# A two-layer attention trunk on one core: hand-ordered vector and scalar queues in the value projection, two of four weight sums added in place by the vector engine

## The chip, the core and the metric

One core of a Trainium2 chip runs the whole program. Its engines work side by side and each takes its own instructions in order: TensorE (PE) multiplies, with weight loads shown as PEld; VectorE (DVE) and ScalarE (ACT) do elementwise work and read the result memory (PSUM); GpSimd (POOL) does elementwise work on SBUF alone and issues accumulating DMAs; SyncE (SP) issues the plain DMAs. The metric is the device time of one execution in microseconds. Everything is float32, multiplied as float32r in two parts: each operand is split into a high part (`hi`, a rounding copy by ACT) and a rest (`lo` = source - `hi`, a subtraction by DVE or POOL), and a product is hi*hi + lo*hi + hi*lo.

## What is computed

Two encoder layers over 512 tokens of width 1024. The stretch at hand is the input projection of the first layer's neighbourhood attention:

```python
xn = rmsnorm(x, norm_g[0])
q, k, v, z = jnp.split(xn @ w_in, 4, axis=-1)     # each 512 x 1024
o = neighbourhood_attention(q, k, v, rpb)          # 16 heads of 64
y = (o * silu(z)) @ w_out
h = x + y
x = h + sigmoid(rmsnorm(h, ple_norm[0]) @ ple_w_gate[0]) * (p[0] @ ple_w_proj[0])
```

The second layer has latent attention in place of `mixer_na`, and a last norm follows.

## The kernel before, in words

`run` first makes `xs` (the transposed, scaled input, in the two tiles `xk[0]` and `xk[1]` of four row blocks each) and its split `xT` (`xh` and `xl`, L1124 to L1128): for each row block DVE scales, ACT copies `xh`, and the rest `xl` is DVE's for the first four blocks and POOL's for the last four. The gate columns `z` come in between (L176, L177). `load_w` (L82 to L84) brings a weight by SP, copies its high part on ACT (`wwhi`) and takes its rest on POOL (`wwlo`).

`values_seven` computes v = xn @ w_v by seven half-size products in place of eight (Strassen's scheme in Winograd's manner, 256 tokens by 512 columns each, in two row halves i). Product p multiplies a left operand by a weight quarter or by a sum of quarters. Products 1, 2 and 4 take `xT` itself. The left operands of 7, 5, 6 and 3 are mixes of `xs`: L1137 adds or subtracts halves of `xk` in place (`d`, by DVE), ACT copies the high part (`h`, L1140) and DVE takes the rest (`l`, L1141). The weights of products 7, 6, 4 and 5 are sums of quarters (T1, T2): a plain DMA brings one quarter and accumulating DMAs, issued by POOL (L248), add the others, W7 = q(1,0) + q(1,2), then W6 = W7 + q(0,0) and W4 = W6 + q(0,2) in the same tile; T2 becomes W5 = q(1,0) + q(0,0). `piece` (L225 to L231) splits half a weight: `whi` by ACT (L229), `wlo` by DVE in two instructions (L231). Raw pieces share three slots (`wraw`) with the weights of `load_w`, and so do the split ones (`whi`, `wlo`).

Each product is 24 matmuls of 128x128 by 128x512 (L277). Products share banks of PSUM: 2 accumulates on 1, 5 and 3 on 6, 4 on 7. So ACT must copy product 1 (`s1`, L285) before product 2 begins; product 7 is added to `s1` and copied to `s17`, product 6 is copied to `s6` and subtracted from 7, and `v_split` (L94, L96) splits finished quarters into the tiles Q. Between the products stand the queries and keys of the first two head pairs: `early(j)`, 48 matmuls (L338), whose results `queries` (ACT L344 and L345, DVE L346 to L353) and `keys` (four copies by ACT, L362 to L365, two rests by DVE, L366 and L367) bring into SBUF.

On PE the order of projection and products is written out: each matmul follows `last_mm`. The sequence is pair 0, product 1, product 2, pair 1, products 7, 6, 4, 5, 3. On ACT, DVE, POOL and SP a planner orders the instructions by its own time model, each engine taking what it reckons ready, earlier source lines first. `issue_after(x)` puts an instruction behind x on its engine.

Of the kernel before, what the change touches and what calls it, by code (L numbers as in the profile page):

```python
# [39 lines left out]

class Trunk:
    def __init__(self, tc, ctx, a, dbg=None):
# [3 lines left out]
        ec = ctx.enter_context  # L46
        self.const = ec(tc.tile_pool(name="const", bufs=1))
# [44 lines left out]
    def split(self, hi, lo, src, scale=1.0):  # L92
        nc = self.nc
        self.last_copy = nc.scalar.activation(hi, src, AF.Copy, scale=scale)  # L94
        if scale == 1.0:
            nc.vector.tensor_tensor(out=lo, in0=src, in1=hi.bitcast(F32), op=ALU.subtract)  # L96
        else:
            nc.vector.scalar_tensor_tensor(lo, src, scale, hi.bitcast(F32), op0=ALU.mult, op1=ALU.subtract)
# [125 lines left out]
    def piece(self, pool, raw, own):  # L224

        nc = self.nc
        hi, lo = ((self.wp if own else pool).tile([P, 1024], F32R, name=t, tag=t if own else "vw", bufs=3 if own else 4)
                  for t in ("whi", "wlo"))
# [5 lines left out]
    def raw_piece(self, n, c, after=None):  # L234
        raw = self.wp.tile([P, 1024], F32, name="wraw", tag="wraw", bufs=3)
        with self.tc.issue_after(after.ins) if after else nullcontext():
            self.nc.sync.dma_start(raw, self.a["na_v"][n, c])
        return raw

    def values_seven(self, pool, xT, X, Q, piece, project):  # L240
# [3 lines left out]
        T = pool.tile([P, 2, 1024], F32, name="T1", bufs=1)  # L244
        first = nc.sync.dma_start(T, quarter(1, 0))
        pool.tile([P, 1024], F32R, name="vw", tag="vw", bufs=4)
        T2 = pool.tile([P, 2, 1024], F32, name="T2", bufs=1)
        add = lambda t, n, c: nc.gpsimd.dma_start(t, quarter(n, c), accum_op=ALU.add, max_dma_last_dim=4096)  # L248
        add(T, 1, 2)
        W, C, s1, s17, s6 = {1: [piece]}, {}, {}, {}, {}  # L250
        made = lambda raw, own: self.piece(pool, raw, own)
# [9 lines left out]
        sub = lambda o, x, y: nc.vector.tensor_tensor(out=o, in0=x, in1=y, op=ALU.subtract)  # L261

        def out(th, n, i, ps):
            self.v_split(Q[th, n][:, 2 * i:2 * i + 2, :], ps)

        def product(p):
            for i in range(2):
                if p in banks:
                    C[p, i] = self.psum(banks[p])
            steps = [(c, i) for c in range(2) for i in range(2)] if p == 1 else [(c, i) for i in range(2) for c in range(2)]  # L270
            for c, i in steps:
                ps = C[base.get(p, p), i]
                m = [(left(p, s, k, i), W[p][c][r][:, k % 2 * S:(k % 2 + 1) * S])
                     for s, r in ((0, 0), (1, 0), (0, 1)) for k in (2 * c, 2 * c + 1)]
                for j, (l, r) in enumerate(m):
                    with self.tc.issue_after(self.last_mm.ins):
                        self.last_mm = nc.tensor.matmul(ps, l, r, start=c == 0 and j == 0 and p in banks,  # L277
                                                        stop=c == 1 and j == 5 and p in (2, 3, 4), skip_group_check=True)
                if c:
                    done(p, i, ps)  # L280

        def done(p, i, ps):
            if p == 1:
                s1[i] = self.temp("s1")
                nc.scalar.activation(s1[i], ps, AF.Copy)  # L285
            elif p == 2:
                out(0, 0, i, ps)
            elif p == 7:
                nc.vector.tensor_tensor(out=ps, in0=ps, in1=s1[i], op=ALU.add)
                s17[i] = pool.tile([P, S], F32, name="s17", tag="s", bufs=3)  # L290
                nc.scalar.activation(s17[i], ps, AF.Copy)
            elif p == 6:
                s6[i] = pool.tile([P, S], F32, name="s6", tag="s", bufs=3)
                nc.scalar.activation(s6[i], ps, AF.Copy)
                sub(C[7, i], C[7, i], s6[i])
            elif p == 4:
                out(1, 0, i, ps)
            elif p == 5:
                q = self.psum("O" if i else "T")
                sub(q, ps, s17[i])  # L300
                sub(ps, ps, s1[i])
                out(1, 1, i, q)
            else:
                out(0, 1, i, ps)

        project(0)
        W[1].append(made(self.raw_piece(0, 1, first), False))
        W[2] = [made(self.raw_piece(0, 2 + c), True) for c in range(2)]
        product(1)
        project(1, True)  # L310
        W[7] = [made(T[:, c, :], c) for c in range(2)]
        product(2)
        add(T, 0, 0)
        project(1, False)
        W[6] = [made(T[:, c, :], True) for c in range(2)]
        product(7)
        add(T, 0, 2)
        nc.sync.dma_start(T2, quarter(1, 0))
        add(T2, 0, 0)
        W[4] = [made(T[:, c, :], False) for c in range(2)]  # L320
        product(6)
        W[5] = [made(T2[:, c, :], True) for c in range(2)]
        product(4)
        W[3] = [made(self.raw_piece(1, 2 + c), not c) for c in range(2)]
        product(5)
        product(3)

    def na_heads(self, pool, xT, zs, Q, XV, weights, piece):
        nc, a = self.nc, self.a
        A, U = {}, {}  # L330

        def load(j):
            weights[j] = [self.load_w(a["na_qk"][i + j], 1024) for i in (0, 8)]
# [7 lines left out]
        def queries(psq):  # L341
            sa = pool.tile([P, S], F32R, name="sa", tag="qs", bufs=4)
            sb = pool.tile([P, S], F32R, name="sb", tag="qs", bufs=4)
            nc.scalar.activation(sa[0:64], psq[0:64], AF.Copy, scale=0.125)  # L344
            nc.scalar.activation(sb[64:128], psq[64:128], AF.Copy, scale=0.125)  # L345
            nc.vector.scalar_tensor_tensor(sa[64:128], psq[0:64], 0.125, sa[0:64].bitcast(F32),  # L346
                                           op0=ALU.mult, op1=ALU.subtract)
            nc.vector.scalar_tensor_tensor(sb[0:64], psq[64:128], 0.125, sb[64:128].bitcast(F32),
                                           op0=ALU.mult, op1=ALU.subtract)
            s0 = []  # L350
            for s in (sa, sb):
                e0 = pool.tile([P, P], F32R, name="s0", tag="s0", bufs=4)
                nc.vector.tensor_copy(e0.rearrange("p (a b) -> p a b", a=2),  # L353
                                      win(s, 0, P, 0, [[448, 2], [1, 64]]).bitcast(F32))
                s0.append(e0)
            return (sa, sb), s0

        def keys(j, psk):
# [3 lines left out]
            nc.scalar.activation(da[0:64], psk[0:64], AF.Copy)  # L362
            nc.scalar.activation(da[64:128], psk[0:64], AF.Copy)
            nc.scalar.activation(db[64:128], psk[64:128], AF.Copy)
            nc.scalar.activation(db[0:64], psk[64:128], AF.Copy)  # L365
# [1013 lines left out]
```

## Time and profile before

| | us |
|---|---|
| median of 3 runs (lowest, highest) | 671.32 (670.32, 671.85) |
| the profiled execution | 669.5 |
| its span, first to last instruction | 667.7 |
| PE busy | 646.0 (97%) |
| DVE, ACT, POOL busy | 429.7, 452.1, 422.2 |

The profile is of one execution. In its timeline a row merges neighbouring instructions of one kind; its second number is the time from the first one's start to the last one's end. Matmuls are pipelined, so eight of them issued every 0.2 us show as one row with the last one's own length at its end. The idle time before a row stands in brackets with what ended it.

### The profile page before, as it was taken

To read this page: it belongs to the slowest core of one execution; us is meant where nothing else is said; L and a number is where in the kernel's file an instruction comes from. 1 tells how busy PE (TensorE), PEld (TensorE's weight loads), DVE (VectorE), ACT (ScalarE), POOL (GpSimd) and SP (SyncE) were. 2 spreads that over 40 slices of the span, in tenths; PEclk is the share of its full clock that TensorE was granted. 3 is DMA by queue.
4 is the path that set the end of the run, shared out by engine and by line. 5 is a ranking of instruction groups with operands and counts; after the bars stand their busy time and mean duration, and the time that the engine had idled before them with its cause. 6 is when DMAs were issued, how large, how long until landed. Compare 5 with 4: busy or idle time off the path is not lost.

```text
span 667.7 us, 9952 instructions
## 1 busy us (share of the span) xinstructions
PE 646.0 (97%) x3299; PEld 543.5 (81%) x3299; DVE 429.7 (64%) x890; ACT 452.1 (68%) x887; POOL 422.2 (63%) x379
## 2 busy tenths in 40 slices
PE   9988987999999999999999999999999999999994
PEld 6866865888888888888899888888888888888884
DVE  6297545476768634567851823788888886374675
ACT  7575444688788754488755544888979898537855
POOL 0493400587987865389844744685978978436974
PEclk9998997999999999999999999999999999999998
DMA  9846853498996898646643425320122213584524
GB/s 323 341 158 189 220 95 94 143 251 209 240 252 168 220 217 257 233 152 200 211 126 122 139 79 142 96 67 9 56 64 64 64 48 132 187 323 132 171 82 158
DMA packets 46100, 107.41 MB, mean 161 GB/s; under 512 B 4705, under 2 KB 17761, under 8 KB 46049
## 3 DMA queue, kind: packets, MB, share of 16 engines
q1 hardware_dynamic: 34032, 85.02, 37.8%
q0 software_dynamic: 11584, 20.97, 15.5%
q10 hardware_dynamic: 432, 0.79, 0.3%
q8 instruction: 26, 0.43, 0.3%
q14 instruction: 26, 0.21, 0.1%
HBM read 95.23 MB, written 25.17 MB: 180 GB/s over the span
## 4 chain that ended last, share of the span: by engine, by line
PE 83%; DMA 8%; ACT 2%; DVE 2%; issue 2%; POOL 2%; POOLq 0%; SPq 0%; DVEq 0%; ACTq 0%
PE ps_mm L107 27%; PE ps_S L107 10%; PE ps_mm L855 7%; PE ps_T L139 6%; PE ps_T L747 5%; PE ps_O L967 4%; PE ps_mm L747 3%; PE ps_S L747 3%; DMA T<-na_v 3%; PE ps_O L504 2%; PE ps_T L107 2%; PE ps_O L107 2%; DMA wraw<-na_z 2%; PE ps_mm L805 2%; PE ps_mm L277 2%
## 5 line engine op out<-in xcount | busy, mean ns | idle before, releaser
L84 POOL TENSOR_TENSOR wwlo<-wraw,wwhi 128x1024 fp32r<-128x1024 f32 (+5 forms) x70 | 123.2, 1772 | 75.2 <-ACT wwhi L83 67.5
L692 POOL TENSOR_TENSOR wlo<-wraw,whi 128x512 fp32r<-128x512 f32 x56 | 72.9, 1335 | 22.3 <-ACT whi L690 20.3
L952 POOL TENSOR_TENSOR ex<-ex,rc 128x512 f32<-128x512 f32 x64 | 66.3, 1043 | 25.8 <-DVE rc L951 21.7
L83 ACT ACTIVATE wwhi<-wraw 128x1024 fp32r<-128x1024 f32 (+5 forms) x73 | 57.1, 805 | 30.6 <-PE ps_mm L107 13.5
L950 ACT ACTIVATE ex<-ps_S,mx 128x512 f32<-128x512 f32 x64 | 44.0, 688 | 11.7 <-DVE mx L948 10.1
L948 DVE TENSOR_REDUCE mx<-ps_S 128x1 f32<-128x512 f32 x64 | 43.7, 683 | 8.2 <-PE ps_S L107 7.5
L96 DVE TENSOR_TENSOR pt_lo<-ps_T,pt_hi 128x512 fp32r<-128x512 f32 x64 | 43.2, 682 | 7.1 <-ACT pt_hi L94 6.7
L478 POOL TENSOR_TENSOR ex<-ex,rc 128x128 f32<-128x128 f32 (+1 forms) x64 | 36.0, 637 | 13.7 <-DVE rc L474 13.7
L94 ACT ACTIVATE pt_hi<-ps_T 128x512 fp32r<-128x512 f32 x64 | 37.7, 595 | 3.3 <-PE ps_T L139 3.0
L139 PE MATMUL ps_T<-ident,ex 128*128 128x128 f32 x256 | 38.3, 272 | 0.0
L139 PEld LDWEIGHTS ps_T<-ident,ex 128*128 128x128 f32 x256 | 31.5, 140 | 7.5
L472 ACT ACTIVATE ex<-ex,mx 128x128 f32<-128x128 f32 (+1 forms) x64 | 30.2, 473 | 9.4 <-DVE mx L462 6.7
L107 PE MATMUL ps_mm<-xh,wwhi 128*128 128x512 f32 x120 | 32.5, 400 | 0.0
L107 PE MATMUL ps_mm<-xh,wwlo 128*128 128x512 f32 x120 | 32.2, 396 | 0.0
L107 PE MATMUL ps_mm<-xl,wwhi 128*128 128x512 f32 x120 | 32.1, 397 | 0.0
L690 ACT ACTIVATE whi<-wraw 128x1024 fp32r<-128x1024 f32 x28 | 29.3, 1056 | 3.2 <-DMA wraw<-sum 2.0
L209 POOL TENSOR_TENSOR u<-u,z 128x512 f32<-128x512 f32 x16 | 22.0, 1372 | 14.4 <-DVE u L205 10.4
L205 DVE TENSOR_TENSOR u<-ps_O,u 64x512 f32<-64x512 f32 x32 | 21.9, 685 | 13.8 <-ACT u L204 13.3
L107 PE MATMUL ps_S<-ko,qo 128*128 128x512 f32 x96 | 28.9, 409 | 0.0
L107 PE MATMUL ps_S<-ke,qe 96*128 96x512 f32 x96 | 28.6, 406 | 0.0
L855 PE MATMUL ps_mm<-cT,wwhi 128*128 128x512 f32 x94 | 27.7, 393 | 0.0
L204 ACT ACTIVATE u<-ps_O 64x512 f32<-64x512 f32 x32 | 19.0, 593 | 12.4 <-PE ps_O L504 9.1
(473 smaller groups left out, 1930.6 us busy)
## 6 DMA issues: line engine op xcount, KB each, us to landing
sum<-gate POOLq DMA_DIRECT2D x12, 1024.0 KB, 8.6
wraw<-na_qk SPq DMA_DIRECT2D x16, 512.0 KB, 4.7
wraw<-sum SPq DMA_DIRECT2D x16, 512.0 KB, 3.3
pe<-pe SPq DMA_DIRECT2D x31, 256.0 KB, 6.1
wraw<-gate SPq DMA_DIRECT2D x12, 512.0 KB, 3.3
T<-na_v POOLq DMA_DIRECT2D x4, 1024.0 KB, 8.9
sum<-sum POOLq DMA_DIRECT2D x4, 1024.0 KB, 10.7
wraw<-na_o SPq DMA_DIRECT2D x8, 512.0 KB, 4.7
```

The lines of the kernel that those rows point to most:

```text
L83: nc.scalar.activation(hi[:, c], raw[:, c], AF.Copy)
L84: f = lambda e, c=c: e.tensor_tensor(out=lo[:, c], in0=raw[:, c], in1=hi[:, c].bitcast(F32), op=ALU.subtract)
L94: self.last_copy = nc.scalar.activation(hi, src, AF.Copy, scale=scale)
L96: nc.vector.tensor_tensor(out=lo, in0=src, in1=hi.bitcast(F32), op=ALU.subtract)
L107: last = self.last_mm = nc.tensor.matmul(out, l, r, start=i == 0, stop=i == n - 1)
L139: self.last_mm = self.nc.tensor.transpose(t[:, i * P:(i + 1) * P], b, self.ident)
L692: nc.gpsimd.tensor_tensor(out=lo[:, o], in0=raw[:, o], in1=hi[:, o].bitcast(F32), op=ALU.subtract)
L747: mm = nc.tensor.matmul(ps, l, r, start=j == 0 and p in banks, stop=j == 11 and p in (2, 3, 4), skip_group_check=True)
L855: self.last_mm = nc.tensor.matmul(PS[key], *terms[i], start=i == 0, stop=i == len(terms) - 1)
L948: nc.vector.reduce_max(mx, sp, axis=AX.X, negate=True)
L950: nc.scalar.activation(ex, sp, AF.Exp, bias=mx, accum_out=sm)
L952: nc.gpsimd.tensor_tensor(out=ex, in0=ex, in1=rc.to_broadcast([P, S]), op=ALU.mult)
```

## The change

- `values_seven` and the query and key steps within it issue their ACT and DVE operations through `InOrder`, which puts each one behind the one before it in the source. `load_w`, POOL's work and the DMAs are not chained. Afterwards the planner orders these engines as before.
- The steps are written out in one sequence (below). The mixes move from `run` into it, spread between the weight pieces, and all stand ahead of `after1`, the copy of product 1. `mix` and `piece` start with ACT's copy and return the rest as a later step.
- W7 and W5 are still made by a plain and an accumulating DMA each. W6 and W4 are made by DVE, which adds raw pieces to W7's tile in place (`sums`), after plain DMAs have brought the pieces.
- `xl` of the last four row blocks is DVE's too.
- The sequence of products ends 7, 6, 5, 4, 3. A pair's queries and keys get both banks first, and `queries` and `keys` are steps of their own. Every product runs by weight halves first, then by row halves.
- The tiles of `xs` and of the raw input lie in the pool `nav`, in the memory that the results Q take later: `more()` makes the two Q tiles that replace `xs`, after the last mix. The other memory at the start of the stretch shifts accordingly.

```diff
+class InOrder:
+    def __init__(self, tc, engine):
+        self.tc, self.engine, self.last = tc, engine, None
+    def __getattr__(self, name):
+        call = getattr(self.engine, name)
+        def run(*args, **kw):
+            with self.tc.issue_after(self.last.ins) if self.last is not None else nullcontext():
+                self.last = call(*args, **kw)
+            return self.last
+        return run
...
-    def piece(self, pool, raw, own):
+    def piece(self, pool, raw):
...
-        nc.scalar.activation(hi, raw, AF.Copy)
-        for o in (slice(0, S), slice(S, 2 * S)):
-            nc.vector.tensor_tensor(out=lo[:, o], in0=raw[:, o], in1=hi[:, o].bitcast(F32), op=ALU.subtract)
-        return hi, lo
+        self.act.activation(hi, raw, AF.Copy)
+        return lambda: [self.rest(hi, lo, raw, o) for o in (slice(0, S), slice(S, 2 * S))] and (hi, lo)
...
+    def mix(self, xk, p):
+        lo, hi = slice(0, 2 * P), slice(2 * P, S)
+        d, y, op = {7: ((0, lo), (0, hi), ALU.subtract), 5: ((0, hi), (1, hi), ALU.subtract),
+                    6: ((1, hi), (0, lo), ALU.add), 3: ((1, lo), (1, hi), ALU.subtract)}[p]
+        d, y = (xk[g][:, :, c] for g, c in (d, y))
+        self.dve.tensor_tensor(out=d, in0=d, in1=y, op=op)
+        t = self.bigtile(f"V{p}")
+        h, l = (t[:, 2 * s:2 * s + 2, :].rearrange("p a (b c) -> p (a b) c", b=2) for s in range(2))
+        self.act.activation(h, d, AF.Copy)
+        return t, lambda: self.dve.tensor_tensor(out=l, in0=d, in1=h.bitcast(F32), op=ALU.subtract)
...
+        def load(p, n, c):
+            T[p] = pool.tile([P, 2, 1024], F32, name=f"W{p}", bufs=1)
+            nc.sync.dma_start(T[p], quarter(1, 0))
+            nc.gpsimd.dma_start(T[p], quarter(n, c), accum_op=ALU.add, max_dma_last_dim=4096)
+        load(7, 1, 2)
...
+        sums = lambda t, i, raw: self.dve.tensor_tensor(out=t[:, i, :], in0=t[:, i, :], in1=raw, op=ALU.add)
...
+        made(1, 0, self.raw_piece(0, 0))
+        rest7 = mixed(7)
+        made(1, 1, self.raw_piece(0, 1), True)
+        load(5, 0, 0)
+        rest7()
+        made(2, 0, self.raw_piece(0, 2))
+        pair.products(0)
+        pair.queries(0)
+        rest5 = mixed(5)
         product(1)
+        p21 = self.piece(None, self.raw_piece(0, 3))
+        rest5()
+        W[2].append(p21())
+        rest6 = mixed(6)
+        pair.keys(0)
+        pair.load(1)
+        rest6()
+        mixed(3)()
+        more()
+        after1(0)
+        after1(1)
+        made(7, 0, T[7][:, 0, :], True)
         product(2)
+        out(0, 0, 0, C[1, 0])
+        out(0, 0, 1, C[1, 1])
+        made(7, 1, T[7][:, 1, :])
+        raws = [self.raw_piece(0, c) for c in both]
+        sums(T[7], 0, raws[0])
+        made(6, 0, T[7][:, 0, :], True)
+        sums(T[7], 1, raws[1])
+        pair.products(1)
+        pair.queries(1)
+        made(6, 1, T[7][:, 1, :])
+        raws = [self.raw_piece(0, 2 + c) for c in both]
+        sums(T[7], 0, raws[0])
+        sums(T[7], 1, raws[1])
+        pair.keys(1)
+        made(5, 0, T[5][:, 0, :])
         product(7)
+        made(4, 0, T[7][:, 0, :], True)
+        after7(0)
+        after7(1)
+        made(5, 1, T[5][:, 1, :])
         product(6)
+        made(4, 1, T[7][:, 1, :], True)
+        after6(0)
+        after6(1)
+        made(3, 0, self.raw_piece(1, 2))
+        product(5)
+        made(3, 1, self.raw_piece(1, 3))
+        after5(0)
+        after5(1)
         product(4)
...
-                (nc.vector, nc.gpsimd)[k // 4].tensor_tensor(out=lo, in0=xs[k], in1=hi.bitcast(F32), op=ALU.subtract)
+                nc.vector.tensor_tensor(out=lo, in0=xs[k], in1=hi.bitcast(F32), op=ALU.subtract)
```

## Rows read from the trace of the kernel before

**Rows 1.** The page: PE's busy time and share, and its granted clock in 40 slices.

```profile
PE 646.0 (97%) x3299; PEld 543.5 (81%) x3299; DVE 429.7 (64%) x890; ACT 452.1 (68%) x887; POOL 422.2 (63%) x379
...
PEclk9998997999999999999999999999999999999998
```

**Rows 2.** View by windows: stretch, busy us by engine, granted clock, DMA share, GB/s.

```profile
99.90:110.00 10.10, 5.52 (x13) 3.83 (x13) 5.52 (x9) 4.43 (x6) 0.00 (x0) 0.67 0.29 58
110.00:124.10 14.10, 14.10 (x62) 11.67 (x63) 7.35 (x11) 7.14 (x10) 5.42 (x3) 0.99 0.36 116
sum 80.20, PE 68.07 PEld 53.22 DVE 48.88 ACT 37.37 POOL 25.56; mean PE 9.72 PEld 7.60 DVE 6.98 ACT 5.34 POOL 3.65
```

**Rows 3.** View of waits, PE: total us, times, longest us.

```profile
PE ps_T L277 <- ACT whi L229: 4.6, 1, 4.6
PE ps_mm L338 <- POOL xl L1128: 4.4, 1, 4.4
PE ps_mm L277 <- DVE lb L367: 1.7, 1, 1.7
```

**Rows 4.** Timeline, PE, pair 0: start, us, engine, line, operation, tiles, count, wait.

```profile
44.12 1.98 PE L338 MATMUL ps_mm<-xh,wwhi 128*128 128x512 f32 x8
...
52.12 0.76 PE L338 MATMUL ps_mm<-xl,wwhi 128*128 128x512 f32 x1 [4.42 <-POOL xl L1128]
...
52.67 3.36 PE L338 MATMUL ps_mm<-xh,wwlo 128*128 128x512 f32 x8
...
55.87 1.98 PE L338 MATMUL ps_mm<-xh,wwhi 128*128 128x512 f32 x8
```

**Rows 5.** Timeline: the third accumulating DMA and product 4 behind it.

```profile
94.97 1.20 POOL L248 DMA_DIRECT2D T<-na_v  x1 [12.18 <-DVE wlo L231]
...
103.31 2.95 ACT L229 ACTIVATE whi<-T 128x1024 fp32r<-128x1024 f32 x3 [4.76 <-DMA T<-na_v]
...
104.42 1.22 PE L277 MATMUL ps_T<-whi,xh 128*128 128x512 f32 x2 [4.57 <-ACT whi L229]
...
109.97 0.83 PE L277 MATMUL ps_T<-whi,xh 128*128 128x512 f32 x2
```

**Rows 6.** Timeline, DVE at the beginning of the stretch.

```profile
39.53 2.49 DVE L1128 TENSOR_TENSOR xl<-xT,xh 128x512 fp32r<-128x512 f32 x4
...
44.33 0.69 DVE L176 TENSOR_TENSOR z<-ps_mm,R 128x512 f32<-128x512 f32 x1
```

**Rows 7.** Timeline, ACT and DVE: one of each step that the change queues.

```profile
42.56 1.06 ACT L229 ACTIVATE whi<-wraw 128x1024 fp32r<-128x1024 f32 x1
...
53.06 1.21 DVE L1137 TENSOR_TENSOR xT<-xT 128x1024 f32<-128x1024 f32 x1
...
54.37 1.06 ACT L1140 ACTIVATE V<-xT 128x1024 fp32r<-128x1024 f32 x1 [2.35 <-DVE xT L1137]
...
58.99 0.69 DVE L346 SCALAR_TENSOR_TENSOR sa<-ps_mm,sa 64x512 fp32r<-64x512 f32 x1
...
60.58 0.22 DVE L353 CAST s<-sb 128x128 fp32r<-128x128 f32 x1
...
61.52 0.59 ACT L362 ACTIVATE da<-ps_mm 64x512 fp32r<-64x512 f32 x1 [2.73 <-PE ps_mm L338]
...
64.66 0.69 DVE L367 TENSOR_TENSOR lb<-ps_mm,db 64x512 fp32r<-64x512 f32 x1
...
67.28 0.60 ACT L285 ACTIVATE s<-ps_S 128x512 f32<-128x512 f32 x1 [0.50 <-PE ps_S L277]
...
73.01 1.29 DVE L231 TENSOR_TENSOR wlo<-T,whi 128x512 fp32r<-128x512 f32 x2 [0.26 <-ACT whi L229]
```

**Rows 8.** Timeline, POOL and DVE at work beside each other.

```profile
40.41 6.70 POOL L1128 TENSOR_TENSOR xl<-xT,xh 128x512 fp32r<-128x512 f32 x3 [1.35 <-ACT xh L1127]
...
47.07 2.79 POOL L84 TENSOR_TENSOR wwlo<-wraw,wwhi 128x1024 fp32r<-128x1024 f32 x1
...
47.58 3.35 DVE L1137 TENSOR_TENSOR xT<-xT 128x1024 f32<-128x1024 f32 x1
```

More of the change, by code (lines that the diff above doesn't have):

```diff
@@ L242, in values_seven @@
+    def values_seven(self, pool, xT, xk, Q, pair, more):
         nc = self.nc
         quarter = lambda n, c: self.a["na_v"][n, c:c + 2].rearrange("c p n -> p c n")
[L244 to L248, printed above, removed]
@@ L269, in product @@
                     C[p, i] = self.psum(banks[p])
[L270 to L304, printed above, removed]
@@ L306, in values_seven @@
-        project(0)
-        W[1].append(made(self.raw_piece(0, 1, first), False))
-        W[2] = [made(self.raw_piece(0, 2 + c), True) for c in range(2)]
-        product(1)
-        project(1, True)
-        W[7] = [made(T[:, c, :], c) for c in range(2)]
-        product(2)
-        add(T, 0, 0)
-        project(1, False)
-        W[6] = [made(T[:, c, :], True) for c in range(2)]
+            for c in range(2):
+                for i in range(2):
+                    ps = C[base.get(p, p), i]
+                    m = [(left(p, s, k, i), W[p][c][r][:, k % 2 * S:(k % 2 + 1) * S])
+                         for s, r in ((0, 0), (1, 0), (0, 1)) for k in (2 * c, 2 * c + 1)]
+                    for j, (l, r) in enumerate(m):
+                        with self.tc.issue_after(self.last_mm.ins):
+                            self.last_mm = nc.tensor.matmul(ps, l, r, start=c == 0 and j == 0 and p in banks,
+                                                            stop=c == 1 and j == 5 and p in (2, 3, 4),
+                                                            skip_group_check=True)
@@ new lines, in after7, with after6, after5 @@
+        def after7(i):
+            self.dve.tensor_tensor(out=C[7, i], in0=C[7, i], in1=s1[i], op=ALU.add)
+            s17[i] = copy("s17", i, C[7, i])
+        def after6(i):
+            s6[i] = copy("s6", i, C[6, i])
+            sub(C[7, i], C[7, i], s6[i])
+        def after5(i):
+            q = self.psum("O" if i else "T")
+            sub(q, C[6, i], s17[i])
+            sub(C[6, i], C[6, i], s1[i])
+            out(1, 1, i, q)
+        made = lambda p, c, raw, vw=False: W.setdefault(p, []).append(self.piece(pool if vw else None, raw)())
@@ new lines, in values_seven, with mixed @@
+        both = range(2)
+        def mixed(p):
+            X[p], rest = self.mix(xk, p)
+            return rest
+        made(1, 0, self.raw_piece(0, 0))
[7 more added lines that the diff above has]
+        rest5 = mixed(5)
+        product(1)
+        p21 = self.piece(None, self.raw_piece(0, 3))
+        rest5()
+        W[2].append(p21())
@@ L321, in values_seven @@
         product(6)
-        W[5] = [made(T2[:, c, :], True) for c in range(2)]
+        made(4, 1, T[7][:, 1, :], True)
[6 more added lines that the diff above has]
+        after5(1)
         product(4)
-        W[3] = [made(self.raw_piece(1, 2 + c), not c) for c in range(2)]
-        product(5)
+        out(1, 0, 0, C[7, 0])
+        out(1, 0, 1, C[7, 1])
         product(3)
-    def na_heads(self, pool, xT, zs, Q, XV, weights, piece):
+        out(0, 1, 0, C[6, 0])
@@ L329, in na_heads @@
+        out(0, 1, 1, C[6, 1])
+    def na_heads(self, pool, xT, zs, Q, xk, weights, more):
         nc, a = self.nc, self.a
         A, U = {}, {}
-        def load(j):
-            weights[j] = [self.load_w(a["na_qk"][i + j], 1024) for i in (0, 8)]
         def product(out, w):
```

128 lines of the change are left out of this document (64 added, 64 removed).

## The prediction

> **What bounds the kernel now.** I read the page's engine shares first. TensorE (PE) is busy 97% of the span, and nearly all of the slices of its granted clock show full speed [rows 1]. So the other engines matter only where PE waits for them. The view by windows then shows where: in the value stretch, 43.9 to 124.1 us, PE is busy 68.07 of 80.20 us, while behind it, from 110 us on, it is busy without a gap [rows 2]. What is gained or lost has to be in the stretch, and the kernel behind it, bound by PE, passes a shift on.
>
> How much is there to gain? Eight matmuls issued back to back take 1.98 us with a last one of 0.39 [rows 4], so (1.98 - 0.39) / 7 = 0.227 us each. The stretch holds 264 of them: two pairs of 48 for queries and keys, and seven products of 24. That is 59.9 us, and with eight short score matmuls of 0.12 us (an estimate from their spacing in the trace) 60.9 us. The first starts at 44.12 us [rows 4], the last ends at about 124.0, so 79.9 - 60.9 = **19.0 us are lost**. The waits of PE name the largest: 4.4 us for POOL's `xl`, 4.6 us for ScalarE's (ACT's) `whi` [rows 3]. Each is followed by the lower of the clock's two levels (1.2 in place of 2.4 GHz; the stretch to 110 us has a granted clock of 0.67 [rows 2]). After the first, the nine matmuls from 52.12 to 55.87 us take 3.75 us where 2.0 would do [rows 4]: 1.7 lost. After the second, twelve take from 104.42 to 109.97 [rows 5], 5.55 us in place of 2.7, a short wait in it: 2.8 lost. A wait for the key rest `lb` is 1.7 [rows 3]. That makes 15.2; some 3.8 lie in smaller waits.
>
> **What the change takes away.** (a) `xl` of the last four row blocks moves from POOL to VectorE (DVE). POOL needs 6.70 us for three of them with DVE busy beside it [rows 8]; DVE makes four in 2.49 [rows 6]. DVE has made the first four by 42.0; four more and one `z` (0.69) bring it to 45.6. PE reads block 4 at about 46.9 and block 7 at 47.5, so the wait of 4.4 and its 1.7 of slow clock go. What covers the four is that the four mixes of `xk`, which follow in DVE's queue before, come later.
>
> (b) The 4.6 us are a DMA. The third accumulating transfer is issued at 94.97, when DVE has read the old sum, and ACT gets the new one at 103.31 [rows 5]. Afterwards the sums for products 6 and 4 are four DVE additions in place (1.21 us each, priced as the 128x1024 operation of L1137 [rows 7]) of pieces that plain DMAs bring ahead. The two DMA sums left, for 7 and 5, start early: their memory lies under tiles of the projection at the start, and nothing in the stretch feeds them. The additions lie in the second half, beside 16.3 us of product 2 and pair 1. So 4.6, its 2.8, and the waits of the same kind at about 91 and 97 us go.
>
> **What it adds: one order for all.** Every ACT and DVE operation of the stretch must now follow the one before it in the source. So a copy can stand behind an unrelated wait. One does: product 2 accumulates into the banks of product 1, so it must wait for the copy `s1`, and `s1` now stands on ACT behind `h3`, the high half of the last mix, which waits for DVE's `d3`. I follow both queues with uncontended durations [rows 6, 7]: a `whi` or `h` 1.06 us, a pair of `wlo` 1.29 (1.2 when the next follows directly), a mix `d` or rest `l` 1.21 (1.14 when the next follows directly, an estimate from what the pairs save), the queries' four DVE pieces 1.81 (58.99 to 60.80), four key copies of 0.59 one behind the other 2.4, then two key rests of 0.69. A hand-over from engine to engine is put at up to 0.1 us (`d6`, which begins at 53.06 and takes 1.21, to its `h` at 54.37), and the times include it.
>
> DVE is free at 45.55 us. `wlo` of W1's first piece to 46.8; `d7` 48.0; `h7` on ACT 49.1, and only then `whi` of W1's second piece, 50.1 (DVE stands 2.1 us); its `wlo` 51.4; `l7` 52.5; W2's first `wlo` 53.7; queries 55.5; `d5` 56.7; `h5` 57.9 (DVE stands 1.2); `l5` 59.1; W2's second `wlo` 60.3; `d6` 61.5; `h6` 62.6; key copies 64.9 (DVE stands 3.5, with `l6` ready behind the key rests); key rests 66.4; `l6` 67.5; `d3` 68.7; `h3` 69.8; `s1` at **70.4**.
>
> PE has no such delay: pair 0 runs 44.12 to 55.0, product 1 to 60.45. Then nothing is left for it: its own order puts product 2 next, and all other products behind. So a hole of 9.95 us opens where the trace of before has none of that size.
>
> **The unknown price** is POOL's. Its 2.4 us weight rests for pair 0's keys and pair 1's queries would fall beside DVE's `xl` and beside `d6` or `d3`. Where POOL's 2.79 us rest ran, `d5` took 3.35 us in place of 1.21 [rows 7, 8]: 2.14 each. Beside the first of POOL's `xl`, however, from 40.41 on, DVE's four took 0.62 each, undisturbed [rows 6, 8]. So the price lies between 0 and 2 x 2.14 = 4.3 us; not below 0, since the chain above has no contention in it to lose. I take half, 2.1, as the rows stand one against one. Product 2 then starts at 72.5 and the hole is 12.05 us.
>
> The Trainium skill speaks against the change here. SBUF — State Buffer, section "Who interferes with whom", states that a DVE instruction with two SBUF inputs and a GpSimd instruction that reads SBUF exclude each other for the whole of the one that came first. By that rule the full 4.3 us count; the row of `d5`, which ends 1.1 us after POOL, agrees, and the four undisturbed `xl` do not.
>
> **From product 2 on** there are 192 matmuls, 43.6 us, and 1.0 of scores. The slow clock after the hole costs 1.7 to 2.8 by the two cases of before [rows 4, 5]; I take 2.2. Following the two queues further, PE is always fed: `wlo` of W7's second piece is done some 8 us before product 7; product 6's second bank comes free, by pair 1's key rests, about 3 us before it is needed; only `s6`, behind the second `whi` of W4, comes about when product 5 wants it. I put 0.5 for such waits; both ends 0 and 3. The sum: 72.5 + 43.6 + 1.0 + 2.2 + 0.5 = 119.8 in place of 124.0, a gain of **4.2 us**. In other words, 19.0 us lost become 12.05 + 2.2 + 0.5 = 14.8.
>
> Moved at no cost: the plain loads of the four raw pieces (four of 0.5 MB in place of two accumulating transfers of 1 MB) stand in SP's queue and wait there for slots that, by the same walk, are free some 7 us ahead of use; if such a load came late, its sum would hold up ACT and DVE, which the 0.5 to 3 covers. Result tiles now lie on the mixes' source and wait for the last mix, long before the first result. Products 5 and 4 change places, with operands of both ready.
>
> The profiled execution took 669.5 us (span 667.7); less 4.2 is 665.3. The median of the three runs, 671.32, is 1.8 above it, so I forecast **667.1 us** for the median.
>
> **Rivals.** *Short hole.* The planner might let the hand order begin before `xl` of the last blocks, and fill DVE's pauses with those. DVE has 16.6 us of work from 45.55 to `d3`; without any pause `s1` would be done at 45.55 + 16.6 + 1.1 + 0.6 + 0.3 of hand-over, 64.2: a hole of 3.8. The loss is then 3.8 + 1.7 + 0.5 = 6.0, the gain 13.0, the time **658.3**. Against it: `l5` needs `h5` and the key rests need four copies on ACT; these pauses, 4.7 us, can't be filled from the chain, and only unchained work could, of which little is left.
>
> *POOL locks DVE out in full.* Product 2 starts at 70.4 + 4.3 = 74.7, the loss is 14.25 + 2.7 = 17.0, the gain 2.0, the time **669.3**. For it: the row of `d5` [rows 8]. Against it: the `xl` rows. It is the rule of the Trainium skill's page named above.
>
> *Slower: pair 1's weights come late.* Their `wwhi` on ACT are not chained; the planner places them by its own times. If it puts them behind `whi` of W6's first piece, which waits for a sum, they end some 14 us after product 2 starts, and PE, which wants them 7.6 us after it (24 x 0.227 and the slow clock), waits 6.3 us and loses some 2.1 more at the low clock: 4.2 - 8.4 = -4.2, **675.5 us**. It decides once they are 5.5 us late with that clock loss included. For it: a planner that reckons with other durations than the chip. Against it: their memory is free, and ACT idle, well before.
>
> **Chances and range.** Forecast 0.59 (own range 664 to 670: P2's price from 0 to 4.3, small waits to 3, less what I can't see behind the stretch); short hole 0.14; POOL in full 0.16; slower 0.11. The range 659 to 672 leaves out most of the first rival and the last. 0.2%, 1.3 us, is what a measurement can tell. Faster by more than that: 0.53 of the forecast, 0.14 of the short hole and 0.10 of POOL in full, 0.77. Within it: 0.06 of the forecast and 0.06 of POOL in full, 0.12. Slower: the last rival's 0.11.
>
> **What would show it.** Right: no wait of PE for `xl`; no wait for a `T` from a DMA; one long wait of PE before product 2's first matmul, for ACT's `s1`, 8 to 14 us, with `h3` just ahead of it on ACT; low clock for 3 to 5 us behind; and no wait above 1 us from there to the end of product 3. Wrong: product 2 following product 1 at once, a wait before pair 1's matmuls, or a loss behind 124 us.

## The result and the profile after

| | before | after |
|---|---|---|
| median, us (runs) | 670.99 (5) | 673.98 (5) |
| ratio of the times, 95% interval | | 1.0042 (1.0028 to 1.0057) |
| span of the profiled execution, us | 667.7 | 671.5 |
| start of the last value matmul, us | 123.6 | 120.5 |
| first transpose of `hg`, the start of the stage behind attention, us | 277.1 | 280.5 |
| the attention stage, between these two, us | 153.5 | 160.0 |

The changed kernel is 0.42% slower. The three lower rows of the table hold the whole result: the value stretch ends 3.1 us earlier than before, and the attention stage behind it takes 6.5 us longer. At `hg` the two traces are 3.4 us apart, at their ends 3.8. In the page of the changed kernel, TensorE (PE) is busy for about as long as in [rows 1], in a longer span, and the granted clock has two new dips, the 6 in the fifth of its 40 slices and the 8 in the tenth, while the 7 in the seventh is gone.

```profile
PE 644.4 (96%) x3299; PEld 544.2 (81%) x3299; DVE 441.1 (66%) x898; ACT 451.5 (67%) x887; POOL 413.3 (62%) x373
...
PEclk9998699998999999999999999999999999999997
```

The waits of PE (total us, times, longest us) show one long wait, the hole, where [rows 3] show three waits, and two new entries behind the stretch, for `Q` and for `pl`. In the new source the value matmuls are L302, the attention's output matmuls L584 and its projections L123. All operations that go through `InOrder` are shown under its line, L51.

```profile
PE ps_S L302 <- ACT s L51: 13.5, 1, 13.5
PE ps_O L584 <- DVE pl L112: 2.1, 1, 2.1
PE ps_mm L123 <- DVE Q L51: 1.3, 1, 1.3
...
PE ps_T L572 <- POOL ex L558: 0.3, 1, 0.3
```

The view by windows, cut at the hole's end and at the end of the stretch (busy us of PE, weight loads, DVE, ACT, POOL; granted clock; DMA share; GB/s), tells the same: PE stands in the first window, works without a gap in the second, and loses 3.8 us in the third. In [rows 2] it is the second half of the stretch in which PE stands.

```profile
43.90:74.36 30.46, 16.92 (x75) 13.70 (x73) 22.46 (x26) 13.38 (x18) 9.76 (x8) 0.83 0.83 242
74.36:120.70 46.34, 46.34 (x200) 38.08 (x201) 31.81 (x55) 24.70 (x34) 6.53 (x3) 0.97 0.33 108
120.70:280.50 159.80, 156.03 (x850) 133.61 (x849) 101.58 (x279) 106.07 (x245) 113.12 (x114) 0.99 0.80 216
```

The hole itself, in the timeline of the changed kernel (start, us, engine, line, operation, tiles, count, wait): 

```profile
39.74 4.29 DVE L1210 TENSOR_TENSOR xl<-xT,xh 128x512 fp32r<-128x512 f32 x7
...
41.92 4.37 POOL L101 TENSOR_TENSOR wwlo<-wraw,wwhi 128x1024 fp32r<-128x1024 f32 x1 [2.94 <-PE ps_S L123]
...
44.55 2.28 DVE L1210 TENSOR_TENSOR xl<-xT,xh 128x512 fp32r<-128x512 f32 x1
...
61.58 2.62 POOL L101 TENSOR_TENSOR wwlo<-wraw,wwhi 128x1024 fp32r<-128x1024 f32 x1 [3.61 <-ACT wwhi L100]
61.92 3.36 DVE L51 TENSOR_TENSOR xT<-xT 128x1024 f32<-128x1024 f32 x1
...
72.63 1.06 ACT L51 ACTIVATE V<-xT 128x1024 fp32r<-128x1024 f32 x1 [3.85 <-DVE xT L51]
...
73.71 1.09 ACT L51 ACTIVATE s<-ps_S 128x512 f32<-128x512 f32 x2
...
74.36 1.22 PE L302 MATMUL ps_S<-whi,xh 128*128 128x512 f32 x2 [13.54 <-ACT s L51]
```

The last three rows are the mechanism that was forecast: `h3`, then `s1` right behind it on ACT, then product 2, at 74.36 in place of 72.5. The rows above them show why it is later. Twice a weight rest of POOL kept a subtraction or a mix of DVE waiting: an `xl` took 2.28 us in place of 0.62 [rows 6], and the mix `d6` 3.36 in place of 1.21 [rows 7].

### The profile page after: what moved, and what is told of

Read it like the earlier page. It is cut to its first block, busy times and chain, and to the rows that moved or that the text cites. A ratio compares the mean times of both kernels' runs of the same rounds, so it can differ in the third digit from the quotient of the medians.

```text
span 671.5 us, 9963 instructions
## 1 busy us (share of the span) xinstructions
PE 644.4 (96%) x3299; PEld 544.2 (81%) x3299; DVE 441.1 (66%) x898; ACT 451.5 (67%) x887; POOL 413.3 (62%) x373
## 4 chain that ended last, share of the span: by engine, by line
PE 85%; DVE 1%; ACT 1%; POOL 1%; issue 0%; POOLq 0%; ACTq 0%
PE ps_mm L123 27%; PE ps_S L123 10%; PE ps_mm L935 6%; PE ps_T L155 6%; PE ps_T L827 5%; PE ps_O L1047 4%; PE ps_mm L827 3%; PE ps_S L827 3%; PE ps_O L584 2%; PE ps_mm L302 2%; PE ps_T L123 2%; PE ps_O L123 2%; PE ps_mm L885 2%; PE ps_T L302 2%; PE ps_mm L407 2%; PE ps_T L572 2%
## 5 line engine op out<-in xcount | busy, mean ns | idle before, releaser
L101 POOL TENSOR_TENSOR wwlo<-wraw,wwhi 128x1024 fp32r<-128x1024 f32 (+5 forms) x70 | 125.7, 1806 | 107.7 <-ACT wwhi L100 90.9
L558 POOL TENSOR_TENSOR ex<-ex,rc 128x128 f32<-128x128 f32 (+1 forms) x64 | 37.4, 674 | 22.0 <-DVE rc L554 21.2
L123 PE MATMUL ps_mm<-xh,wwhi 128*128 128x512 f32 x120 | 35.1, 417 | 1.3 <-DVE Q L51 1.3
L123 PE MATMUL ps_mm<-xl,wwhi 128*128 128x512 f32 x120 | 32.1, 396 | 0.0
L123 PE MATMUL ps_mm<-xh,wwlo 128*128 128x512 f32 x120 | 31.5, 395 | 0.0
L123 PE MATMUL ps_S<-ko,qo 128*128 128x512 f32 x96 | 28.9, 409 | 0.0
L123 PE MATMUL ps_S<-ke,qe 96*128 96x512 f32 x96 | 28.6, 406 | 0.0
```

What stands on the lines that cost most here:

```text
L101: f = lambda e, c=c: e.tensor_tensor(out=lo[:, c], in0=raw[:, c], in1=hi[:, c].bitcast(F32), op=ALU.subtract)
L123: last = self.last_mm = nc.tensor.matmul(out, l, r, start=i == 0, stop=i == n - 1)
```

## The experiments

Each comparison below is with the kernel before on the same chip (medians of 670.8 to 671.2 us). Beside each time stand the start of the last value matmul and the length of the attention stage, from there to the first transpose of `hg`. These two are read from the one execution that was profiled, which isn't the median one: it took 657.9 us for e6 and 671.9 for e8, 2.6 and 1.5 us less than their medians, and in the others it lies within 1 us.

| run | median, us | ratio (95% interval) | last value matmul | attention stage |
|---|---|---|---|---|
| the changed kernel | 673.98 | 1.0042 (1.0028 to 1.0057) | 120.5 | 160.0 |
| e1: `s1` ahead of mixes 6 and 3 | 666.29 | 0.9926 (0.9912 to 0.9941) | 113.8 | 158.4 |
| e2: row halves first in all products but 1 | 667.0 | 0.9937 (0.9920 to 0.9955) | 121.3 | 153.4 |
| e3: small casts on ACT | 669.54 | 0.9978 (0.9968 to 0.9987) | 121.0 | 154.0 |
| e5: before, all `xl` on DVE | 666.71 | 0.9937 (0.9919 to 0.9955) | 121.2 | 153.5 |
| e6: no hand order | 660.51 | 0.9836 (0.9812 to 0.9860) | 106.7 | 158.4 |
| e7: e6 and row halves first | 655.52 | 0.9768 (0.9751 to 0.9785) | 109.3 | 153.4 |
| e8: before, weight halves first | 673.38 | 1.0043 (1.0028 to 1.0058) | 125.8 | 152.7 |
| e9: e6, sums for 6 and 4 by DMA | 665.57 | 0.9922 (0.9905 to 0.9940) | 114.4 | 158.4 |
| e10: small casts with a result-memory operand | 669.61 | 0.9979 (0.9966 to 0.9993) | 121.2 | 155.5 |
| e11: e7 and the casts of e10 | 655.19 | 0.9763 (0.9735 to 0.9790) | 109.3 | 153.7 |
| e12: e1 and e2 together | 661.3 | 0.9854 (0.9826 to 0.9882) | 114.3 | 153.4 |
| e13: row halves first in product 3 alone | 666.9 | 0.9932 (0.9908 to 0.9956) | 121.5 | 153.4 |

Two theories stood for the attention stage. By the first, the stage loses time through something that the change put at its beginning, and would still pass a shift on. By the second, the stage is bound by something else than PE and gives every shift back. The column on the right decides. Leave out the runs that change the casts or the halves of the kernel before (e3, e8, e10, e11). With the stretch ending anywhere from 106.7 to 123.6, the stage then has one of two lengths, about 153.5 or 158.4 to 160.0, and which one doesn't go by when it begins. So the second theory is out: the stage passes a shift on.

**The order of the halves.** In the changed kernel every product works through weight halves first. Before, all but product 1 took row halves first. This was put back in all products but the first (e2), and then in the last product alone (e13):

```diff
-            for c in range(2):
-                for i in range(2):
+            for a in range(2):
+                for b in range(2):
+                    c, i = (a, b) if p == 1 else (b, a)
```

For e13 the condition reads `p != 3`.

> All products but the first run row half by row half again, as in the kernel before; the rest is the changed kernel. Theory A: the 1.28 us that PE waits at the stretch's end for a bank (for DVE's split of the last result) come from both halves of product 3 ending within 1.4 us; now the first half ends 2.7 us ahead, the wait goes, 1.0 to 1.5 us are gained (672.5 to 673). Rival: the wait comes from the first head's exponentials, which stand ahead of the split on ACT; then it stays at about 1 us or more.

> The changed kernel with row halves first in product 3 alone, the last of the seven; products 2, 7, 6, 5 and 4 stay weight halves first. Theory (the attention stage loses because both row halves of the last product finish together, and with them the order in which DVE takes the steps behind): the wait for Q of 1.3 us and the wait for pl of 2.1 us both gone, attention stage of 153 to 154 us in place of 160.0, and the time of the run with all row halves first, 666.5 to 668.5 us. A cast of about 3.8 us beside two subtractions of POOL may well stay, with no matmul waiting for it. Rival (the order of the earlier products matters as much, or the cast alone makes the wait): the wait for pl stays, attention stage of 157 us or more, 670 to 673 us.

Both brought the attention stage to 153.4 us, with the hole still there (13.5 and 13.6 us). From e2, 1.0 to 1.5 us had been expected, for the wait at the border alone; it gave 7.0. So the order of 24 matmuls, those of product 3, is worth all of the loss behind the stretch: 674.0 - 666.9 = 7.1 us by the medians. How it is lost shows at two places. The first is the border. In the changed kernel, the first row half of product 3 is complete only six matmuls before the second, and by then the exponentials of head 0 stand ahead of the split on ACT:

```profile
118.86 1.28 ACT L552 ACT_TABLE_LOAD   x1
...
120.15 0.40 ACT L552 ACTIVATE ex<-ex,mx 128x128 f32<-128x128 f32 x1
...
122.03 0.57 ACT L51 ACTIVATE Q<-ps_mm 128x512 fp32r<-128x512 f32 x1
...
122.64 0.69 DVE L51 TENSOR_TENSOR Q<-ps_mm,Q 128x512 fp32r<-128x512 f32 x1
...
123.48 1.85 PE L123 MATMUL ps_mm<-xh,wwhi 128*128 128x512 f32 x7 [1.28 <-DVE Q L51]
```

PE needs the bank that this split empties. In e13 the first row half is complete twelve matmuls before the second. It is split while PE still works on the other, behind two of head 0's exponentials in place of four, and no wait is left:

```profile
119.42 0.58 ACT L51 ACTIVATE Q<-ps_mm 128x512 fp32r<-128x512 f32 x1
120.03 0.69 DVE L51 TENSOR_TENSOR Q<-ps_mm,Q 128x512 fp32r<-128x512 f32 x1 [0.32 <-ACT Q L51]
```

The second place is 30 us further on, in the queue of DVE of the changed kernel:

```profile
149.07 1.39 DVE L422 CAST s<-sa 128x128 fp32r<-128x128 f32 x1
...
150.22 0.86 POOL L706 DMA_DIRECT2D sum<-gate  x1
...
150.97 3.83 DVE L422 CAST s<-sb 128x128 fp32r<-128x128 f32 x1
151.02 1.37 POOL L229 TENSOR_TENSOR ol<-u,oh 128x512 fp32r<-128x512 f32 x1
...
152.27 2.43 POOL L101 TENSOR_TENSOR wwlo<-wraw,wwhi 128x1024 fp32r<-128x1024 f32 x1
...
154.72 0.68 DVE L112 TENSOR_TENSOR pl<-ps_T,ph 128x512 fp32r<-128x512 f32 x1
...
155.45 0.39 PE L584 MATMUL ps_O<-pl,Q 128*128 128x256 f32 x1 [2.11 <-DVE pl L112]
```

A cast that takes 0.22 us undisturbed [rows 7] lasts 3.83: it ends at 154.80, when the second of two subtractions of POOL that follow each other has ended, at 154.70. `pl` stands behind it, and PE waits 2.1 us for `pl`. In e13 the cast takes as long, but `pl` is ahead of it, and nobody waits:

```profile
149.61 0.68 DVE L112 TENSOR_TENSOR pl<-ps_T,ph 128x512 fp32r<-128x512 f32 x1
150.21 3.87 DVE L423 CAST s<-sb 128x128 fp32r<-128x128 f32 x1
150.36 1.31 POOL L229 TENSOR_TENSOR ol<-u,oh 128x512 fp32r<-128x512 f32 x1
151.60 2.39 POOL L101 TENSOR_TENSOR wwlo<-wraw,wwhi 128x1024 fp32r<-128x1024 f32 x1
```

So the collision is there in both. What differs is which of two DVE instructions the planner puts first. That the order of product 3's halves turned this order round follows from e13, since nothing else was changed. By which step of the planner's reckoning it did so is not shown.

**The cast.** Two runs take the cast away from the collision: ACT makes it (e3), or DVE makes it with the result bank, times zero, as a second operand (e10).

```diff
-                self.dve.tensor_copy(e0.rearrange("p (a b) -> p a b", a=2),
-                                      win(s, 0, P, 0, [[448, 2], [1, 64]]).bitcast(F32))
+                cut = lambda t: win(t, 0, P, 0, [[448, 2], [1, 64]])
+                self.dve.scalar_tensor_tensor(e0.rearrange("p (a b) -> p a b", a=2), cut(psq), 0.0,
+                                              cut(s).bitcast(F32), op0=ALU.mult, op1=ALU.add)
```

> In the attention stage the small copies s0 of pairs 2 to 7 are made by ACT in place of DVE (those of pairs 0 and 1, in the stretch, stay); the rest is the changed kernel. Theory A: the copy of 3.83 us, shut out by POOL's two subtractions at 151 to 154.7 us, goes; with it go PE's wait of 2.11 us for pl and the low clock behind it (1.8 us): 669.5 to 670.5. Rival (any other order that the planner finds brings another such collision): a wait of 1 to 3 us elsewhere in the attention stage, time 672 to 675.

> The changed kernel with the attention's small casts made by DVE with the result bank as a second operand (multiplied by zero and added), so that the operation has one operand in SBUF and is no plain SBUF copy. Theory (the 3.83 us of one cast of some 0.2 us is DVE shut out of SBUF by two subtractions of POOL in a row): no such cast above 0.8 us, mean of a cast below 500 ns in place of 1049 to 1354, no wait of PE for pl, and its 2.1 us and the slow clock of some 1.8 behind it gone; the wait for Q of 1.3 us stays. 669.5 to 670.5 us. Rival (POOL's reading holds up any DVE operation with an operand in SBUF, or the wait is one of order): casts stay above 800 ns in the mean and a wait of about 2 us shows again, 672 to 675 us.

In both the wait for `pl` is gone and the one of 1.3 us for `Q` stays. 4.4 us come back by the medians, and 6.0 and 4.5 of the stage's length. The groups of casts from 120 to 280 us, first of the changed kernel and then of e10 (last of its columns: busy us and mean ns, idle time before them):

```profile
L422 DVE CAST s<-sb 128x128 fp32r<-128x128 f32 x6 | 8.1, 1354 | 0.1
L422 DVE CAST s<-sa 128x128 fp32r<-128x128 f32 x6 | 6.3, 1049 | 0.2
```

```profile
L423 DVE SCALAR_TENSOR_TENSOR s<-ps_mm,sa 128x128 fp32r<-128x128 f32 x6 | 1.7, 290 | 0.2
L423 DVE SCALAR_TENSOR_TENSOR s<-ps_mm,sb 128x128 fp32r<-128x128 f32 x6 | 1.7, 276 | 0.0
```

All twelve of e10 lie between 271 and 292 ns, though six of them began while a weight rest of POOL was running. Here are a cast of the changed kernel and one of e10, each begun 2.0 us after a weight rest of 2.96 us. The first ends with POOL's subtraction, the second doesn't wait for it:

```profile
165.71 2.96 POOL L101 TENSOR_TENSOR wwlo<-wraw,wwhi 128x1024 fp32r<-128x1024 f32 x1
...
167.71 1.05 DVE L422 CAST s<-sa 128x128 fp32r<-128x128 f32 x1
```

```profile
210.67 2.96 POOL L101 TENSOR_TENSOR wwlo<-wraw,wwhi 128x1024 fp32r<-128x1024 f32 x1
...
212.68 0.29 DVE L423 SCALAR_TENSOR_TENSOR s<-ps_mm,sa 128x128 fp32r<-128x128 f32 x1
```

In e3 and e10 the planner's order on PE is not quite that of the changed kernel either, and a part of their gain may be due to that.

**Weight halves first in the kernel before.** If the order of the halves alone makes the border wait, it should do so in the kernel before too.

```diff
-            steps = [(c, i) for c in range(2) for i in range(2)] if p == 1 else [(c, i) for i in range(2) for c in range(2)]
+            steps = [(c, i) for c in range(2) for i in range(2)]
```

> The kernel before with one line of the change: every product runs weight half by weight half, as only the first did. Theory A (this loop order by itself costs at the end of the stretch and, by the planner's order behind it, in the attention stage): a wait of 1 to 1.5 us for the split of the last result, and perhaps the collision of the small copy with POOL; 672 to 677 us against 670.9. Rival (the cost needs the first head's work to stand ahead on ACT, which only the changed kernel has): within 1 us of 670.9.

The time rose by 2.6 us, nearly as much as by the whole change, but at another place: the stretch ends 2.2 us later, at 125.8, and the attention stage is 152.7 us long, without a wait for `Q` or `pl`. In place of the 4.6 us for `whi` and the 1.7 for `lb` [rows 3] PE has these waits in the stretch:

```profile
PE ps_mm L277 <- DVE lb L367: 3.1, 1, 3.1
PE ps_T L277 <- DVE ps_T L261: 2.5, 1, 2.5
```

All waits of PE in the stretch add up to nearly the same, 12.2 us and 12.0 before. But the granted clock is now low behind both of these two, 0.68 from 98 to 107 us and 0.66 from 107 to 112, where before it was low behind one (0.67, [rows 2]). The ten runs spread from 671.6 to 675.0 us, and the profile is of one of 671.9; what the longer ones lose is not shown.

So the order of halves needs a partner for the border wait. In the kernel before and in e8, head 0's first bias is asked for at 123.42 and 124.30 us, at the end of the last product, and its exponentials come behind the last split. In the changed kernel DVE already works with the bias at 117.0 us, and the exponentials come ahead of that split. That this is the partner is argued from the order, not tested by itself.

**The hole.** Two runs take the cause of the hole away: e1 keeps the hand order and moves `after1(0)` and `after1(1)` up, and e6 leaves the order out.

```diff
         W[2].append(p21())
+        after1(0)
+        after1(1)
         rest6 = mixed(6)
...
-        after1(0)
-        after1(1)
         made(7, 0, T[7][:, 0, :], True)
```

```diff
-            self.act, self.dve = InOrder(self.tc, nc.scalar), InOrder(self.tc, nc.vector)
```

> The two copies of product 1 (s1) move ahead of the mixes 6 and 3 in ACT's hand-written order; nothing else changes. Theory A (the hole before product 2 is the place of s1 in ACT's order, and the attention stage behind passes a gain on): s1 ends about 61 us in place of 74.3, PE waits under 1 us before product 2, the low clock behind it goes (2 us), DVE becomes the limit later in the stretch, which ends at 108 to 112 us in place of 120.7; time 662 to 667 us, against 674.0 of the changed kernel and 671.0 before. Theory B (the attention stage is held by something else than PE, which is why 3.1 us gained in the stretch became 3.4 lost): the stretch ends as much earlier, but the attention stage takes as much longer, and the time stays within 671 to 675.

> The changed kernel with the same sequence in the source, but ACT and DVE unchained, so that the planner orders them. Theory A (the written order makes the hole): s1 is copied when product 1 is done, PE waits at most 3 us before product 2, and some small waits come back; stretch ends at 108 to 114, time 662 to 668. Rival (DVE has too much work before product 2 in any order, since it now makes all rests and the mixes here): the weights of product 2 or the mixes are late, PE waits 4 us or more before product 2 or 7, time 668 to 674.

Either way the hole goes (waits for `s1` of 0.6 and 1.5 us). So it was the place of `s1` in the written order, as forecast. Against the changed kernel e1 gains 7.7 us and e6 13.5. In e1 the stretch ends at 113.8, later than the 108 to 112 expected. What e1 doesn't gain is a second wait of the same making, which had been hidden behind the hole. The waits of PE and the timeline of e1:

```profile
PE ps_mm L302 <- DVE lb L51: 3.7, 1, 3.7
PE ps_O L584 <- DVE pl L112: 2.1, 1, 2.1
```

```profile
85.85 2.35 DVE L51 TENSOR_TENSOR W<-W,wraw 128x1024 f32<-128x1024 f32 x2
...
88.93 0.69 DVE L51 TENSOR_TENSOR lb<-ps_mm,db 64x512 fp32r<-64x512 f32 x1
...
89.77 2.04 PE L302 MATMUL ps_mm<-whi,V 128*128 128x512 f32 x4 [3.66 <-DVE lb L51]
```

The two weight sums for product 4 stand ahead of pair 1's key rests in the source, and product 6 waits for the bank that these rests empty. The granted clock is at its lower level of 1.2 GHz from about 89.8 to 95 us, which costs about 2.6 us more. In e6 there is no wait for `lb`.

**The parts.** e5 makes only the first part of the change, in the kernel before. e9 gives the sums for products 6 and 4 back to accumulating DMAs, in e6.

```diff
-                (nc.vector, nc.gpsimd)[k // 4].tensor_tensor(out=lo, in0=xs[k], in1=hi.bitcast(F32), op=ALU.subtract)
+                nc.vector.tensor_tensor(out=lo, in0=xs[k], in1=hi.bitcast(F32), op=ALU.subtract)
```

```diff
-        raws = [self.raw_piece(0, c) for c in both]
-        sums(T[7], 0, raws[0])
+        nc.gpsimd.dma_start(T[7], quarter(0, 0), accum_op=ALU.add, max_dma_last_dim=4096)
...
-        sums(T[7], 1, raws[1])
...
-        raws = [self.raw_piece(0, 2 + c) for c in both]
-        sums(T[7], 0, raws[0])
-        sums(T[7], 1, raws[1])
+        nc.gpsimd.dma_start(T[7], quarter(0, 2), accum_op=ALU.add, max_dma_last_dim=4096)
```

> The kernel before with one line of the change: DVE makes all eight rests xl, none is POOL's. Theory A (this term of the sum was right: PE's wait of 4.4 us and 1.7 us of low clock behind it go, and the rest of the kernel passes it on): 665 to 667 us against 670.9 before. Rival (what is gained is waited for again at the sums that DMAs make, whose start does not move with PE): those waits grow from 4.6 us to 8 or more, time 669 to 672.

> The changed kernel with ACT and DVE unchained and with the sums for products 6 and 4 made by accumulating DMAs in W7's tile again, in place of DVE's additions. Theory A (DVE's sums are what takes the waits for T away): PE waits 4 us or more for a W that a DMA brings, with low clock behind it, 665 to 669 us against 660.5. Rival (the new sequence of products, 7, 6, 5, 4, gives each DMA sum a product more to hide behind, and DVE's additions are not needed): no such wait above 1.5 us, 659 to 662 us.

One line of the kernel before, `xl` on DVE, is worth 670.8 - 666.7 = 4.1 us, about as much as the prediction gave the whole change. A part of what the wait for `xl` cost comes back in the wait for `whi` at product 1's and 2's banks, 3.0 us in place of 0.7. The sums by DVE are worth 665.6 - 660.5 = 5.1 us. The wait of PE for a weight, expected with DMAs, is not there; PE waits 3.6 us for `s6`, ACT's copy of product 6. On ACT that copy stands behind a `whi` that waited 3.3 us for a DMA's sum:

```profile
93.42 1.06 ACT L244 ACTIVATE whi<-W 128x1024 fp32r<-128x1024 f32 x1 [3.28 <-DMA W<-na_v]
...
95.81 0.59 ACT L311 ACTIVATE s<-ps_mm 128x512 f32<-128x512 f32 x1
```

**Together.** e12 has both repairs in the hand order. e7 is the version without hand order and with row halves first, and e11 has the casts of e10 besides.

> The hand order kept, the two copies s1 moved ahead of mixes 6 and 3, and row halves first in all products but the first. Theory (the hole and the loss of the attention stage are two separate causes and add up): no wait for s1 above 1 us, attention stage of 153 to 154 us in place of 158.4, the wait for lb of 3.7 us and its slow clock as with the copies alone, 666.3 - 5.0 = 661.3, so 660 to 663 us. Rival (one loss hides the other): 665 to 667 us.

> The changed kernel with ACT and DVE unchained and with all products but the first run row half by row half. Theory A (the row-half order takes away both the wait at the stretch's end and the collision behind it, whatever the stretch does): no wait for the last split, no wait for pl, attention stage 5 to 7 us shorter than without it: 654 to 657 us, against 660.5 with the weight-half order. Rival (the two waits went away by chance of the planner's order in that one kernel): a wait of 1 us or more comes back in the attention stage, 658 to 662 us.

> The version without the hand order and with the row halves first in products 7, 6, 5, 4 and 3 (655.5 us), with the same cast. Theory: with row halves first PE waits for no cast any more, so it gains little: attention stage 153 us, 654 to 656 us. Rival (the planner makes another order of the whole for it, and the order matters more than the cast): more than 657 us, with new waits of PE in the stretch or behind it.

e12 gains 12.7 us on the changed kernel. Taken singly the repairs gain 7.7 and 7.0, together 14.7, but 1.6 of e1's are the slow clock behind `pl` that e1 doesn't have (below), which e2 takes away too. With that part counted once, the hole and the loss behind the stretch are two causes that add up. PE still waits 2.3 us for `lb` and 2.2 for a copy `s`. e7 is 2.3% faster than the kernel before; its PE waits for 2.6 us at `s1` and for nothing else above 1 us. The casts bring e11 nothing that can be measured (0.3 us, the intervals lie on each other), since with row halves first nobody waits for them. The hand order, against the planner's own, costs 661.3 - 655.5 = 5.8 us even after both repairs.

## Why the prediction was wrong

It forecast 667.1 us and a gain, and the time is 673.98, a loss. By its steps:

- **The waits that go.** Right. No wait for `xl` is left and none for a weight from a DMA.
- **The hole.** Right in place and cause, and too short: product 2 begins at 74.36, 1.9 us later than forecast, behind a hole of 13.54 us in place of 12.05. One start in it is wrong by its own terms: 42.0, four `xl` and one `z` make 45.2 for DVE, not 45.55. In the trace two `z` stood there, and DVE's first `wlo` began at 47.36. The term that was mis-sized is POOL's price, taken at 2.1 of at most 4.3. It measured (2.28 - 0.62) + (3.36 - 1.21) = 3.8. So that term went by the rival "POOL locks DVE out in full". The four undisturbed `xl` [rows 6, 8], on which the half was founded, were misread: there DVE had come first, and it was POOL that paid, with 6.70 us for three. The row at 41.92 us shows this side again: POOL's rest takes 4.37 us in place of 2.4, while DVE's `xl` run on. The rule of the Trainium skill (SBUF — State Buffer, "Who interferes with whom") says that whichever of the two comes first keeps the other out. These rows agree with it, on both sides, and show more: three of the seven `xl` from 39.74 us on, 0.61 us each, began after POOL's rest at 41.92 and still ran ahead of it.
- **The slow clock behind the hole.** 2.2 forecast. From 74.36 to 77.72 us eight matmuls took 3.36 us in place of 8 x 0.227 = 1.82, 1.5 lost.
- **No waits from product 2 to the end of product 3.** Right: none, where 0.5 was forecast. The stretch ends 3.1 us earlier, of 4.2 forecast.
- **"The kernel behind it, bound by PE, passes a shift on."** This is the step that failed, and with it an edit that the prediction never priced: "every product runs by weight halves first". The step was read from the kernel before, where PE is busy without a gap behind the stretch, and that shows only that nothing was late in that order. A shift as such is passed on (the stage is 158.4 us long in e1 and e6, which begin it at 113.8 and 106.7). What failed is that the change would leave the stage itself as it was; the sum has no term for it. The attention stage became 6.5 us longer: 1.3 for `Q`, 2.1 for `pl`, 1.6 of slow clock behind the latter, and some 1.5 that no wait above 0.3 us accounts for. e13 undoes this edit in one product and comes out at 666.9 us.

So with that one order put back, the forecast time is met to 0.2 us. That is closer than the steps deserve: in the profile of e13 `hg` begins 2.2 us earlier than before, where the medians give a gain of 4.1 (the execution profiled was 1.5 us faster than the median before, and 0.8 slower in e13). The range ended at 672, since every case in it kept the stage behind as it was, though "a loss behind 124 us" stood among the signs of an error.

Of the other rivals, the short hole didn't occur: the hand order began behind the last `xl`, and DVE stood in the pauses of the prediction's walk, 2.1 and 3.5 us in the two longest. The slower one, pair 1's weights late, didn't either: PE has no wait there. The place where the time was lost was in none of the rivals.

Still open are the 1.5 us mentioned, and why the planner turns the order of `pl` and the cast round.

## What to carry to other kernels

An edit that changes in which order results become complete, at the same work, has to be priced at the border of the next stage: look up who splits or copies the last result, what stands ahead of it on that engine, and who waits for its memory. A written order for in-order queues is only as good as its worst place: for every copy that frees a bank, ask what stands ahead of it and what that waits for, and move the copy up. Where DVE and POOL subtract beside each other, count the one that comes second as held up for the whole of the other, at times for two or three in a row. Count a tiny cast of DVE as held up too, and keep it from standing ahead of what PE waits for.

## What the runs showed of the hardware that was not expected

A DVE cast of 0.22 us lasted 3.83 us (3.87 in e13) beside two POOL subtractions in a row of 1.37 and 2.43 us. It did not get in between the two. The same section of the Trainium skill names casts among the operations that can contend with GpSimd, and both rows agree. That the first comer keeps the other out can't be read from them: by the recorded starts the cast began 0.05 us (0.15 in e13) ahead of the first subtraction, while POOL was issuing a DMA.

A wait of PE of about 2.1 us, for the same `pl`, lowered the granted clock in one kernel and not in three others. One-microsecond windows, first of the changed kernel, then of e1:

```profile
154.00:155.00 1.00, 0.00 (x0) 0.00 (x0) 1.00 (x2) 0.19 (x1) 0.70 (x1) 1.00 1.00 406
155.00:156.00 1.00, 0.55 (x4) 0.55 (x5) 0.95 (x6) 0.05 (x1) 0.00 (x0) 0.97 0.85 320
156.00:157.00 1.00, 1.00 (x7) 1.00 (x6) 0.99 (x4) 1.00 (x5) 0.00 (x0) 0.50 0.89 229
```

```profile
147.00:148.00 1.00, 0.00 (x0) 0.00 (x0) 1.00 (x1) 0.50 (x1) 1.00 (x1) 1.00 1.06 430
148.00:149.00 1.00, 0.25 (x2) 0.25 (x3) 0.99 (x5) 0.00 (x0) 0.01 (x1) 1.00 1.00 385
149.00:150.00 1.00, 1.00 (x10) 1.00 (x10) 0.97 (x5) 0.75 (x3) 0.00 (x0) 1.00 0.90 148
```

PE stood for as long and on the same instruction in both. The changed kernel then ran at a granted clock of 0.50 (1.2 GHz) to about 159.2 us and lost some 1.6 us, and e1 none; e6 and e9, with the same wait, keep a granted clock of 1.00 behind it as e1 does. That is the difference between stages of 160.0 and of 158.4 us. So what a short wait costs can't be read from its length alone.
